# A fused layer kernel: the mixer stage's loads, stores and projection blocks in another order

## The chip, the cores and the metric

The kernel runs on one core of one Trainium2 chip. A core has five engines, each with an instruction queue of its own that is worked through in order: TensorE (PE, matrix products; the profile keeps its weight loads apart as PEld), VectorE (DVE), ScalarE (ACT), GpSimd (POOL) and SyncE (SP), which here issues every DMA. The metric is the device time of one execution in microseconds (us); of several executions the median is given.

## The reference

One layer of a diffusion backbone works on 128 context tokens and 2048 latent tokens, 1024 features each. After a modulated RMS norm, one projection feeds a short gated convolution (512 features) and a bidirectional mLSTM with four heads of 128; both meet in an output projection, and a gated feed-forward network (FFN) with a convolution follows. Cut to what the change touches:

```python
h = rmsnorm(x, norm1) * (1 + scale1) + shift1
sc_b, sc_c, sc_x, q, k, v, o, g = jnp.split(h @ w_in, idx, axis=-1)
u = (sc_c * sc_x).reshape(B, rows, row_len, D_CONV)
y_sc = sc_b * conv3(u, conv_sc_w, conv_sc_b, axis=2).reshape(B, T, D_CONV)
h_m, C, n, m = mlstm_bidir(heads(q), heads(k), heads(v), gates, C0, n0, m0)
h_m = h_m * lax.rsqrt(jnp.mean(h_m * h_m, axis=-1, keepdims=True) + EPS)
h_m = h_m * mh_norm.reshape(N_HEADS, HEAD_DIM).astype(jnp.float32)
h_m = h_m.reshape(B, T, D_MLSTM).astype(x.dtype) * jax.nn.sigmoid(o)
x = x + gate1 * (jnp.concatenate([y_sc, h_m], axis=-1) @ w_out)
h2 = rmsnorm(x, norm2) * (1 + scale2) + shift2
```

The mLSTM runs over 17 chunks of 128 tokens (chunk 0 is the context), forward and backward. Weights and activations are fp32; each product is made of three matmuls on high and low parts of its operands.

## The kernel before

Tokens stand in six blocks (0 to 5) of 384, the last of 256. A **block product** (`gemm`, lines 221 to 223) is one 128-row weight tile against one block: 8 slices times 3 matmuls, 24 in all, into one of two `acc` buffers. Its weight tile is loaded (line 119, two `wst` buffers), copied to its high part on ACT (line 127) and reduced to its low part on POOL in two halves (line 130).

The program's stages in order:

1. Start: modulation vectors, first norms, the v and gate projections of blocks 3 to 5 (`vg`), then block products of those three blocks for k, q, short convolution and o (`heads`, `shortconv`). Beside these, a generator `side` is advanced one step for each block product: `first_stats` sums the squares of blocks 0 to 2 on ACT and DVE (lines 177 to 181) and takes their inverse norms through PE, DVE and POOL (`inv_rms`, lines 144 to 148); then `mod_dve` makes 32 modulation vectors on DVE (two instructions of 1024 columns at line 661 and a small one at line 663 for each).
2. `vg` and the k heads of blocks 0 to 2 around the gate phase.
3. **Sums**: 34 units, one for each chunk and pair of heads, going backwards. A unit transposes k on PE (line 891), weighs v on DVE (895), multiplies on PE (902) and stores the state (918). Between units stand block products taken from a generator `fill`.
4. **Mix**: 34 units going forwards. `weave` writes one step for each unit; in it, stages of neighbouring units stand in a fixed order. For step i: `rows` (a 512 KB broadcast load of R, line 940) of unit i+2, `load` (k2, v2, q2, sb; lines 869, 874, 934) of unit i+1, the o gate load and the y store (869, 1031), the mask of unit i+1 on POOL (945), the products with R of unit i-1 on PE (976, 978), the scores of unit i (957), the transposes of unit i-3 (1021), and on DVE, ACT and POOL the denominators, head sums, norm and exponentials. After them `fill` gives block products.
5. The FFN: the out projection's last block products stand beside `sums`, which combines normalised rows for the FFN (spread at line 252, DVE at 272 to 284); then FFN up (1198 to 1200), then down (1352 to 1354).

`fill` in the kernel before is one chain: 12 block products for q, 12 for o, 36 for the short convolution of blocks 0 to 2 (12 weight tiles, three tiles at a time for three blocks each), and 32 of the 48 steps of `out_proj`. An `out_proj` step k loads the x row of step k+2 (line 553), multiplies (221 to 223), adds into the row on DVE (597), and at the beginning of step k+1 `close` stores that row (559), squares it on ACT (564) and adds the square on DVE (565). `next_y` brings in the y of the next blocks (504, 515, 516). `stats` (491 to 493) turns the summed squares of two blocks into inverse norms.

What sets the order: in Sums and before, a scheduler orders each engine's queue when the program is built. From the first Mix instruction to the end of `out_proj`, `in_order(first)` pins every engine to the order in which the code is written. `pa` gives two `acc` buffers; Mix has one PSUM bank for scores, two for y, and one (`st`) for transposes; k2 and q2 have three buffers, v2 and sb four, R four.

## Time and profile before

| | |
|---|---|
| Median of 3 runs | 2556.18 us (2555.6 to 2556.26) |
| The profiled execution | 2555.41 us, of which its span 2553.6 us |
| Mean granted TensorE clock | 0.987 of full speed |

Read the profile from PE: the page's first part gives each engine's busy share, its second part where in the span that share falls, and the fourth the chain that ended last. Of one execution, 1.8 us lie outside the span. Times in the span count from its first instruction.

### The profile page before, as it was taken

To read this page: it belongs to the slowest core of one execution; us is meant where nothing else is said; L and a number is where in the kernel's file an instruction comes from. 1 tells how busy PE (TensorE), PEld (TensorE's weight loads), DVE (VectorE), ACT (ScalarE), POOL (GpSimd) and SP (SyncE) were. 2 spreads that over 40 slices of the span, in tenths; PEclk is the share of its full clock that TensorE was granted. 3 is DMA by queue.
4 is the path that set the end of the run, shared out by engine and by line. 5 is a ranking of instruction groups with operands and counts; after the bars stand their busy time and mean duration, and the time that the engine had idled before them with its cause. 6 is when DMAs were issued, how large, how long until landed. Compare 5 with 4: busy or idle time off the path is not lost.

```text
span 2553.6 us, 42517 instructions
## 1 busy us (share of the span) xinstructions
PE 2469.7 (97%) x16127; PEld 2363.8 (93%) x16127; DVE 1664.1 (65%) x2738; ACT 1107.2 (43%) x2035; POOL 560.4 (22%) x467
## 2 busy tenths in 40 slices
PE   8999999999999889899999999899999999999998
PEld 8899999999999888899999999788888899999998
DVE  3992552322367666678678666877777786787586
ACT  4511143222255544455455444645555554443342
POOL 2531243111243333332112111121122100000000
PEclk9999999999999999999999999999999999999999
DMA  7772873255477776875225222522222277766674
GB/s 276 254 274 87 290 246 117 94 170 166 145 234 247 257 244 202 292 241 173 80 71 177 83 83 83 172 105 85 84 91 99 70 241 218 247 205 220 187 222 131
DMA packets 281423, 444.60 MB, mean 174 GB/s; under 512 B 23282, under 2 KB 206722, under 8 KB 279554
## 3 DMA queue, kind: packets, MB, share of 16 engines
q1 hardware_dynamic: 281218, 441.88, 53.0%
q8 instruction: 127, 2.08, 0.3%
q14 instruction: 78, 0.64, 0.1%
HBM read 335.31 MB, written 106.48 MB: 173 GB/s over the span
## 4 chain that ended last, share of the span: by engine, by line
PE 77%; DVE 9%; DMA 5%; issue 3%; ACT 3%; POOL 2%; SPq 1%; DVEq 0%; ACTq 0%; POOLq 0%
PE acc L221 7%; PE acc L223 7%; PE acc L222 7%; PE pa L1198 6%; PE pa L1200 6%; PE pa L1199 6%; PE d L1353 5%; PE d L1354 5%; PE d L1352 5%; PE pb L1198 3%; PE pb L1200 3%; PE pb L1199 3%; PE pc L1198 2%; PE pc L1199 2%; PE pc L1200 2%
## 5 line engine op out<-in xcount | busy, mean ns | idle before, releaser
L221 PE MATMUL acc<-hH,wh 128*128 128x384 f32 (+1 forms) x1536 | 515.6, 336 | 11.4 <-DVE row L597 11.1
L223 PE MATMUL acc<-hH,wl 128*128 128x384 f32 (+1 forms) x1536 | 507.5, 330 | 0.1
L222 PE MATMUL acc<-hL,wh 128*128 128x384 f32 (+1 forms) x1536 | 507.1, 330 | 0.0
L1352 PE MATMUL d<-bh,wh 128*128 128x272 f32 x1232 | 356.4, 290 | 0.7 <-ACT raw L1210 0.7
L1354 PE MATMUL d<-bh,wl 128*128 128x272 f32 x1232 | 356.8, 290 | 0.0
L1353 PE MATMUL d<-bl,wh 128*128 128x272 f32 x1232 | 356.2, 289 | 0.0
L1198 PE MATMUL pa<-tH,wh 128*128 128x288 f32 (+1 forms) x1056 | 347.8, 329 | 5.4 <-DVE raw L1212 2.9
L130 POOL TENSOR_TENSOR wl<-wst,wh 128x512 fp32r<-128x512 f32 (+1 forms) x160 | 236.6, 1500 | 518.8 <-ACT wh L127 497.3
L1200 PE MATMUL pa<-tH,wl 128*128 128x288 f32 (+1 forms) x1056 | 346.7, 328 | 1.0 <-DVE wl L331 1.0
L1199 PE MATMUL pa<-tL,wh 128*128 128x288 f32 (+1 forms) x1056 | 346.5, 328 | 0.0
L331 POOL TENSOR_TENSOR wl<-st,wh 128x512 fp32r<-128x512 f32 x132 | 185.7, 1408 | 695.5 <-ACT wh L330 655.2
L221 PEld LDWEIGHTS acc<-hH,wh 128*128 128x128 f32 x1536 | 293.3, 191 | 15.0 <-issue 10.5
L222 PEld LDWEIGHTS acc<-hL,wh 128*128 128x128 f32 x1536 | 292.8, 191 | 0.3 <-issue 0.2
L223 PEld LDWEIGHTS acc<-hH,wl 128*128 128x128 f32 x1536 | 292.2, 190 | 0.9 <-POOL wl L130 0.6
L1141 DVE SCALAR_TENSOR_TENSOR tt<-raw,fw,tt 128x127 f32<-128x127 f32 (+4 forms) x264 | 245.7, 952 | 3.7 <-ACT tt L1147 2.7
L1352 PEld LDWEIGHTS d<-bh,wh 128*128 128x128 f32 x1232 | 232.6, 189 | 1.3 <-ACT raw L1210 1.1
L1353 PEld LDWEIGHTS d<-bl,wh 128*128 128x128 f32 x1232 | 232.6, 189 | 0.2
L1354 PEld LDWEIGHTS d<-bh,wl 128*128 128x128 f32 x1232 | 232.5, 189 | 0.0
L1198 PEld LDWEIGHTS pa<-tH,wh 128*128 128x128 f32 x1056 | 198.4, 188 | 22.3 <-ACT c L1205 2.6
L1200 PEld LDWEIGHTS pa<-tH,wl 128*128 128x128 f32 x1056 | 199.0, 188 | 17.0 <-DVE wl L331 1.4
L1199 PEld LDWEIGHTS pa<-tL,wh 128*128 128x128 f32 x1056 | 198.6, 188 | 15.6
L330 ACT ACTIVATE wh<-s 128x512 fp32r<-128x512 f32 x176 | 110.8, 630 | 175.5 <-PE pc L1199 86.2
(243 smaller groups left out, 4834.0 us busy)
## 6 DMA issues: line engine op xcount, KB each, us to landing
st<-in_w_up SPq DMA_DIRECT2D x88, 512.0 KB, 3.8
us<-uD SPq DMA_DIRECT2D x48, 544.0 KB, 4.6
wst<-in_w_in SPq DMA_DIRECT2D x48, 512.0 KB, 3.7
uD<-tt SPq DMA_DIRECT2D x44, 544.0 KB, 2.7
R<-nD SPq DMA_DIRECT2D x34, 512.0 KB, 6.0
wm<-in_w_modr SPq DMA_DIRECT2D x32, 512.0 KB, 5.1
wst<-in_w_out SPq DMA_DIRECT2D x24, 512.0 KB, 5.6
st<-wsD SPq DMA_DIRECT2D x32, 384.0 KB, 3.3
```

Of the source, the lines that this page charges most:

```text
L130: G.tensor_sub(wl[:, a:a + n // 2], st[:, a:a + n // 2], wh[:, a:a + n // 2].bitcast(F32))
L221: PE.matmul(acc[:, :n], w_h, hH[:, k, :n], start=(k == 0), stop=False)
L222: PE.matmul(acc[:, :n], w_h, hL[:, k, :n], start=False, stop=False)
L223: PE.matmul(acc[:, :n], w_l, hH[:, k, :n], start=False, stop=(k == KT - 1))
L331: (G if on_pool else V).tensor_sub(wl, a, wh.bitcast(F32))
L1141: V.scalar_tensor_tensor(o, i, w, o, op0=ALU.mult, op1=ALU.add)
L1198: PE.matmul(acc, wh[:, w], rh, start=(kk == 0 and i in (0, 1, 5)), stop=False, skip_group_check=True)
L1199: PE.matmul(acc, wh[:, w], rl, start=False, stop=False, skip_group_check=True)
L1200: PE.matmul(acc, wl[:, w], rh, start=False, stop=(kk == 3), skip_group_check=True)
L1352: PE.matmul(acc, wh[:, c], uh, start=(kk == 0), stop=False)
L1353: PE.matmul(acc, wh[:, c], ul, start=False, stop=False)
L1354: PE.matmul(acc, wl[:, c], uh, start=False, stop=(kk == KH - 1))
```

## The change

Seven edits, most of them in Mix and around it.

- **o gate:** `head` multiplies the sigmoid by the head norm factor `mhn` on ACT (one more instruction for each of the 24 o block products); Mix then multiplies both heads in one DVE instruction (`third`) in place of two.
- **norm:** the mean's factor goes into the ACT square, and the addition of EPS moves from DVE to POOL.
- **Mix loads:** `load` stands two steps ahead, before `rows`.
- **Sums:** `load` two steps ahead, the second product two steps behind, three buffers for kT and vw.
- **Block products:** Sums gets the 24 of q and o, 0.65 for each step; Mix begins the short convolution and gets 1.6 for each step, where before Sums had one and Mix one with a second every third step from step 9 on. Sums goes from 38 to 24 block products and Mix from 48 to 60. Of `out_proj`, 26 steps stood in Mix and 22 behind it; now it is 24 and 24.
- **out_proj:** a row is stored and squared two steps after its product, and its square added a step later; `stats` five steps after a group's end rather than two.
- **first_stats:** three steps of `mod_dve` between the squares of a block and its inverse norm.

```diff
             S.activation(r[:, :n], acc[:, :n], func, scale=scale)
+            if func == AF.Sigmoid:
+                S.activation(r[:, :n], r[:, :n], AF.Copy, scale=mhn[:, h:h + 1])
             Q.dma_start(dst[h][:, t0:t0 + n], r[:, :n])
...
                 t0, n = BL[b]
-                ss = sss[b]
                 Q.dma_start(xD[m][:, t0:t0 + n], xr[:, :n])
                 if m == 0:
-                    S.activation(ss[:, :n], xr[:, :n], AF.Square)
+                    second = b in grps[1]
+                    sq = sss[b] = (rq if second else ssp).tile([P, 384], F32, name="cr" if second else "ss")
                 else:
                     sq = sqp.tile([P, 384], F32, name="sq")
-                    S.activation(sq[:, :n], xr[:, :n], AF.Square)
-                    V.tensor_add(ss[:, :n], ss[:, :n], sq[:, :n])
-
-            rows, got, behind, held, sss, past = [], [], [], [], {}, set()
+                S.activation(sq[:, :n], xr[:, :n], AF.Square)
+                return b, m, sq
+
+            def add(b, m, sq):
+                n = BL[b][1]
+                if m:
+                    V.tensor_add(sss[b][:, :n], sss[b][:, :n], sq[:, :n])
+
+            rows, got, behind, squared, held, sss, past = [], [], [], [], [], {}, set()
             for k in range(2):
...
                 grp, (t0, n) = grps[g], BL[b]
-                if k % 16 == 0:
-                    sss.update((b, ssp.tile([P, 384], F32, name="ss")) for b in grp)
-                    if g + 1 < len(grps):
-                        ny = next_y(grps[g + 1], (lambda: True, lambda b=grp[0]: (b, KT - 1) in past))
-                for x in behind:
-                    close(*x)
+                if k % 16 == 0 and g + 1 < len(grps):
+                    ny = next_y(grps[g + 1], (lambda: True, lambda b=grp[0]: (b, KT - 1) in past))
                 load_r(k + 2)
+                while squared:
+                    add(*squared.pop())
+                if len(behind) > 1:
+                    squared.append(close(*behind.pop(0)))
                 if k + 4 < len(steps):
...
                     del ws[:2]
-                if held and k == held[0] + 2:
-                    stats(*held[1:])
+                if held and k == held[0] + 5:
+                    stats(held[1], [sss[b] for b in held[1]])
                     held = []
...
                 past.add((b, m))
-                behind = [(b, m, xr)]
+                behind.append((b, m, xr))
                 if k % 16 == 15:
                     run(ny)
-                    if k == len(steps) - 1:
-                        close(*behind.pop())
-                        defer.append(lambda: stats(grp, [sss[b] for b in grp]))
-                    else:
-                        held = [k, grp, [sss[b] for b in grp]]
+                    held = [k, grp]
+                if k == len(steps) - 1:
+                    for x in squared + [close(*x) for x in behind]:
+                        add(*x)
+                    defer.append(lambda: stats(grp, [sss[b] for b in grp]))
                 yield
...
-            def first_stats():
+            def first_stats(mod):
+
                 for b in BA:
...
                     yield
+                    yield from islice(mod, 3)
                     inv_rms(ss, BL[b][1], rcol(b))
...
             late()
-            side = chain(first_stats(), mod_dve(), down_sums())
+            mod = mod_dve()
+            side = chain(first_stats(mod), mod, down_sums())
             run(vg((3,), hs, ws), prep(4))
...
                     PE.transpose(ps[:, h * P:(h + 1) * P], self.k2[:, h], ident)
-                self.kT = ms.tile([P, 256], F32, name="kT", bufs=2)
+                self.kT = ms.tile([P, 256], F32, name="kT", bufs=3)
                 S.activation(self.kT, ps[:, :256], AF.Copy)
-                self.vw = ms.tile([P, 2, 2, 129], F32, name="vw", bufs=2)
+                self.vw = ms.tile([P, 2, 2, 129], F32, name="vw", bufs=3)
                 V.tensor_tensor(self.vw, bc(self.v2[:, :, None, :], [P, 2, 2, 129]),
...
                 for h in range(2):
-                    S.activation(sj, hv[:, h], AF.Square, accum_out=ss[:, h:h + 1])
+                    S.activation(sj, hv[:, h], AF.Square, scale=QS, accum_out=ss[:, h:h + 1])
...
                 ss = self.ss
-                V.tensor_scalar(ss, ss, 1.0 / P, EPS, op0=ALU.mult, op1=ALU.add)
+                G.tensor_scalar(ss, ss, EPS, None, op0=ALU.add)
                 G.tensor_tensor(ss, ss, mhalf[:, :2], op=ALU.pow)
...
             def third(self):
-                hp, o2 = self.hp, self.o2
-                for h in range(2):
-                    V.scalar_tensor_tensor(o2[:, h], self.psT[:, h * P:(h + 1) * P], mhn[:, 2 * hp + h:2 * hp + h + 1], o2[:, h],
-                                           op0=ALU.mult, op1=ALU.mult)
+                o2 = self.o2
+                V.tensor_tensor(o2, self.psT[:, :256].rearrange("p (h t) -> p h t", h=2), o2, op=ALU.mult)
...
-        def weave(units, fill, extra, stages):
+        def weave(units, fill, rate, stages):
...
                 if -1 <= i < n + 3:
-                    next(fill, None)
-                    if extra and i >= 9 and i % extra == 0:
+                    for _ in range(int((i + 2) * rate) - int((i + 1) * rate)):
                         next(fill, None)
...
         outs = out_proj(((0, 1), (2, 3), (4, 5)), late, wo)
-        fill = chain(heads(BA, hs, 12, qD, AF.Copy, QS), heads(BA, hs, 20, oD, AF.Sigmoid, 1.0),
-                     shortconv(BA, hs, load_y, [I["w_out"][m] for m in range(2)], wo), islice(outs, 32))
+        fill = chain(heads(BA, hs, 12, qD, AF.Copy, QS), heads(BA, hs, 20, oD, AF.Sigmoid, 1.0))
         with tc.tile_pool(name="ms", bufs=1, side="right") as ms:
-            weave([Sums(c, hp) for c in range(NL - 1, -2, -1) for hp in range(2)], fill, 0,
-                  ((-1, "second"), (0, "first"), (1, "load")))
+            weave([Sums(c, hp) for c in range(NL - 1, -2, -1) for hp in range(2)], fill, 0.65,
+                  ((-2, "second"), (0, "first"), (2, "load")))
+        run(fill)
+        fill = chain(shortconv(BA, hs, load_y, [I["w_out"][m] for m in range(2)], wo), islice(outs, 37))
         mb = phr.enter_context(tc.tile_pool(name="mb", bufs=1, side="right"))
         first = len(nc.cur_bb.bb.instructions)
-        weave([Mix(c, hp) for c in range(-1, NL) for hp in range(2)], fill, 3,
-              ((2, "rows"), (1, "load"), (-2, "gate"), (-4, "last"), (1, "mask"),
+        weave([Mix(c, hp) for c in range(-1, NL) for hp in range(2)], fill, 1.6,
+              ((2, "load"), (2, "rows"), (-2, "gate"), (-4, "last"), (1, "mask"),
                (-1, "out"), (0, "scores"), (-3, "turn"), (0, "queries"), (-2, "norm"), (-1, "denom"), (0, "weigh"),
```

Three places where the order of the instructions changes:

**The inverse norms of blocks 0 to 2, on POOL, in the start stage.** `rc` is the inverse norm, `wl` a half of a weight's low part: two halves for each weight tile, a tile for three block products on PE. Before:

```order
L130 TENSOR_TENSOR wl<-wst,wh 128x512 x2
L148 TENSOR_TENSOR rc<-rc,mhalf 128x3
L130 TENSOR_TENSOR wl<-wst,wh 128x512 x2
L148 TENSOR_TENSOR rc<-rc,mhalf 128x3
L130 TENSOR_TENSOR wl<-wst,wh 128x512
L148 TENSOR_TENSOR rc<-rc,mhalf 128x3
```

After:

```order
L130 TENSOR_TENSOR wl<-wst,wh 128x512 x2
L148 TENSOR_TENSOR rc<-rc,mhalf 128x3
L130 TENSOR_TENSOR wl<-wst,wh 128x512 x4
L148 TENSOR_TENSOR rc<-rc,mhalf 128x3
L130 TENSOR_TENSOR wl<-wst,wh 128x512 x3
L148 TENSOR_TENSOR rc<-rc,mhalf 128x3
```

The three inverse norms stand further apart. On PE the three groups of sums of squares (line 144) stood after 2, 4 and 6 block products of the k heads, and now stand after 5, 10 and 15.

**The first weights of the short convolution of blocks 0 to 2, on SP, at the end of Sums.** `wst` is a weight tile, `row` a finished block product of o. Before, the third of these weights stands among the loads and stores of Sums, nine block products ahead of the convolution's first:

```order
L403 DMA oD_65<-row_5686 128x384
L918 DMA sD_67<-sb_5599 128x516
L874 DMA v2_5908<-vD_66 128x258
L119 DMA wst_6166<-in_w_in 128x1024
L403 DMA oD_65<-row_5740 128x384
```

After, all three stand behind the store of the last block product of Sums (row_6356, from acc_6331); the PE instruction behind acc_6331 is the first product with the weight wst_6385:

```order
L950 DMA R_6370<-nD_68 128x1024
L879 DMA k2_6372<-kD_63 128x2x128
L884 DMA v2_6374<-vD_66 128x258
L879 DMA q2_6376<-qD_64 128x2x128
L950 DMA R_6378<-nD_68 128x1024
L405 DMA oD_65<-row_6356 128x384
L119 DMA wst_6385<-in_w_in 128x1024
L119 DMA wst_6392<-in_w_in 128x1024
L119 DMA wst_6399<-in_w_in 128x1024
```

The weights moved from the middle of Sums to its end, behind a store.

**A step of Mix with an out projection block, on DVE.** `sq` is the squared row, `ss` their sum, `acc` the block product, `hL` the low part of the next y. Before:

```order
L966 TENSOR_TENSOR R_8669<-S_8913,R_8669 128x2x256
L1026 SCALAR_TENSOR_TENSOR o2_8770<-st_8916,mhn_133,o2_8770 128x128 x2
L1001 SCALAR_TENSOR_TENSOR hv_8931<-y_8904,den_8924,hv_8931 128x128 x2
L565 TENSOR_TENSOR ss_8510<-ss_8510,sq_8947 128x384
L516 TENSOR_TENSOR hL_8958<-xt_8859,hH_8957 128x384 x4
L597 SCALAR_TENSOR_TENSOR row_8820<-acc_8967,modT_85,row_8820 128x384
```

After:

```order
L976 TENSOR_TENSOR R_8943<-S_9188,R_8943 128x2x256
L1035 TENSOR_TENSOR o2_9035<-st_9191,o2_9035 128x256
L1011 SCALAR_TENSOR_TENSOR hv_9205<-y_9179,den_9199,hv_9205 128x128 x2
L572 TENSOR_TENSOR ss_8866<-ss_8866,sq_9122 128x384
L518 TENSOR_TENSOR hL_9130<-xt_9089,hH_9129 128x384 x4
L604 SCALAR_TENSOR_TENSOR row_9080<-acc_9239,modT_85,row_9080 128x384
```

The addition keeps its place ahead of the read of `acc`, but its square sq_9122 now belongs to an earlier step's ACT work (sq_8947 was made in the same step); and one instruction takes the place of two at the o gate.

## Prediction

> **What bounds the kernel now.** The page's first and fourth parts come first: busy time by engine, and the chain that ended last.
>
> ```profile
> span 2553.6 us, 42517 instructions
> ...
> PE 2469.7 (97%) x16127; PEld 2363.8 (93%) x16127; DVE 1664.1 (65%) x2738; ACT 1107.2 (43%) x2035; POOL 560.4 (22%) x467
> ...
> PE 77%; DVE 9%; DMA 5%; issue 3%; ACT 3%; POOL 2%; SPq 1%; DVEq 0%; ACTq 0%; POOLq 0%
> ```
>
> PE is busy for 2469.7 of 2553.6 us, so 84 us of idle time, and whatever PE loses at a lower clock, is all that this change can win; it takes no matmul away. Next comes busy time by stretch: the end of the start stage, Sums (two rows), Mix, the out projection behind it, and the FFN. The columns are the stretch, its length, busy time of PE, PEld, DVE, ACT, POOL, granted clock, DMA share and GB/s.
>
> ```profile
> 114.00:133.00 19.00, 13.56 (x75) 13.16 (x74) 18.86 (x34) 5.71 (x11) 8.04 (x5) 0.82 0.70 246
> 497.00:677.00 180.00, 180.00 (x1021) 174.62 (x1020) 47.59 (x107) 48.58 (x110) 32.84 (x22) 1.00 0.52 154
> 677.00:694.00 17.00, 17.00 (x98) 16.91 (x97) 4.16 (x9) 6.12 (x13) 2.58 (x2) 1.00 0.59 198
> 694.00:1005.00 311.00, 282.61 (x1825) 278.93 (x1823) 206.26 (x515) 154.87 (x489) 118.43 (x103) 0.97 0.75 238
> 1005.00:1121.00 116.00, 102.93 (x620) 99.09 (x620) 76.85 (x129) 49.91 (x95) 42.78 (x32) 0.94 0.80 270
> 1121.00:2553.00 1432.00, 1410.01 (x9358) 1322.25 (x9358) 1058.86 (x1468) 688.39 (x1027) 207.86 (x156) 0.99 0.44 144
> ```
>
> Sums has no idle PE time and can only lose. Mix has 28.4 us of it, the out projection 13.1, the start 5.4. The FFN's 22 us lie behind everything that changes; I leave them as they are. So the sum has four terms.
>
> **Term 1, the start: -8.1 us.** PE's groups, DVE's groups and PE's rows in the start stage, and the stretch in which the granted clock was 0.50:
>
> ```profile
> L144 PE MATMUL st<-ones,ss 128*128 128x1 f32 x18 | 3.0, 280 | 5.4 <-DVE modT L663 4.7 <-DVE rc L147 0.8
> ```
> ```profile
> L661 DVE SCALAR_TENSOR_TENSOR y<-wm,cB 128x1024 f32<-128x1024 f32 x25 | 34.4, 1375 | 0.3
> L181 DVE TENSOR_TENSOR ss<-ss,sq 128x384 f32<-128x384 f32 x15 | 11.8, 791 | 0.0
> ```
> ```profile
> 109.83 0.34 PE L221 MATMUL acc<-hH,wh 128*128 128x384 f32 x1
> ...
> 112.82 0.34 PE L223 MATMUL acc<-hH,wl 128*128 128x384 f32 x1
> ```
> ```profile
> 126.15:132.98 6.83, 5.31 (x19) 5.34 (x20) 6.73 (x12) 0.00 (x0) 0.96 (x1) 0.50 1.02 369
> ```
>
> PE waits 5.4 us for DVE at the sums of squares, and the 5.31 us of work behind it run at half the clock, which costs 2.7: together 8.1. Each sum now comes five block products after the one before, not two. The two PE rows stand 17 matmuls apart, 0.176 us each, so a block product of 24 takes 4.2 us, one of 256 tokens about two thirds of that (2.9), and five take 18.8 us on average. In that time DVE has, from an inverse norm to the last addition of the next block, seven additions (5.5 us) and six multiplications by the modulation weights (8.3): 13.8 us, a few small instructions beside. I take the whole 8.1. Bounds: -8.1, and -3 if DVE, which is full in this stretch, still comes 5 us late once.
>
> **Term 2, Mix: -31 us.** PE's groups between 694 and 1005 us with their idle time, and the half-clock stretches:
>
> ```profile
> L221 PE MATMUL acc<-hH,wh 128*128 128x384 f32 x361 | 126.5, 350 | 4.4 <-DVE row L597 4.4
> L978 PE MATMUL y<-v,R 128*128 128x129 f32 x272 | 52.9, 280 | 5.4 <-issue 2.6 <-DVE R L966 1.5 <-ACT hv L999 1.1
> ...
> L957 PE MATMUL S<-q,k 128*128 128x128 f32 x136 | 22.0, 287 | 15.3 <-DMA q<-qD 15.3
> ```
> ```profile
> 877.08:883.91 6.83, 4.17 (x15) 4.20 (x16) 6.76 (x15) 0.62 (x2) 3.21 (x3) 0.50 0.99 311
> 911.22:914.63 3.41, 3.41 (x14) 3.41 (x13) 3.41 (x4) 0.00 (x0) 3.41 (x4) 0.50 0.87 258
> 948.76:952.18 3.42, 3.42 (x18) 3.42 (x18) 0.73 (x3) 2.88 (x12) 0.00 (x0) 0.50 0.77 253
> 959.00:962.42 3.42, 3.17 (x10) 3.20 (x11) 3.34 (x13) 0.86 (x4) 0.74 (x1) 0.50 0.65 195
> 1006.79:1010.20 3.41, 3.41 (x13) 3.41 (x12) 2.96 (x3) 1.66 (x5) 2.84 (x2) 0.50 0.00 0
> ```
>
> The half-clock PE time is 17.6 us and costs 8.8; with 28.4 idle, Mix gives at most 37.2. More than half of the idle time is the scores' wait for q. The timeline shows one such wait:
>
> ```profile
> 870.41 0.75 SPq L869 DMA_DIRECT2D q<-qD  x1
> ...
> 879.74 0.55 PE L957 MATMUL S<-q,k 128*128 128x128 f32 x1 [6.74 <-DMA q<-qD]
> ```
>
> From issue to use it is 9.3 us, and one step of Mix is 311/34 = 9.1 us: a load one step ahead cannot make it when the DMA engines are full. SP also stands before it, for rows not yet written, and DVE for their squares:
>
> ```profile
> SPq L559 <- DVE row L597: 57.9, 11, 8.6
> ```
> ```profile
> L565 DVE TENSOR_TENSOR ss<-ss,sq 128x384 f32<-128x384 f32 x18 | 10.1, 558 | 44.0 <-ACT sq L564 44.0
> ```
>
> Waits of SP at the row stores: 57.9 us in 11, the longest 8.6. With loads two steps ahead (18 us) and a row stored two block products after it was made, both the 15.3 and SP's 57.9 should go. DVE's 44.0 us at the addition stand ahead of the next read of `acc`, and so of PE's 4.4; with the square a step old the addition finds it ready, and the 4.4 go. Behind these two waits come the clock stretches at 877, 911 and 959 (10.75 us, so 5.4). That is 25.1. Of the other 8.7 us (R, hv, issue) and the two remaining stretches (3.4) I let half go: 6. Bounds: everything (-37), and -19 (q's wait and half of what came with it).
>
> [...] The timeline before the stretch at 959:
>
> ```profile
> 959.25 0.66 PE L221 MATMUL acc<-hH,wh 128*128 128x384 f32 x1 [2.40 <-DVE row L597]
> ```
>
> [...]
>
> **Term 3, a new start-up wait between Sums and Mix: +10 us.** The first three short-convolution weights stand on SP behind the store of the last block product of Sums, and the next instruction of PE needs the first of them. The chain's links, from ACT's and POOL's groups in Sums, the page's DMA issues and SP's timeline:
>
> ```profile
> L402 ACT ACTIVATE row<-acc 128x384 f32<-128x384 f32 x21 | 10.2, 485 | 49.2 <-PE acc L223 49.2
> L127 ACT ACTIVATE wh<-wst 128x1024 fp32r<-128x1024 f32 x10 | 10.6, 1058 | 35.5 <-PE acc L222 32.2 <-issue 3.3
> L130 POOL TENSOR_TENSOR wl<-wst,wh 128x512 fp32r<-128x512 f32 x21 | 31.2, 1502 | 129.1 <-ACT wh L127 129.1
> ```
> ```profile
> wst<-in_w_in SPq DMA_DIRECT2D x48, 512.0 KB, 3.7
> ...
> wst<-in_w_out SPq DMA_DIRECT2D x24, 512.0 KB, 5.6
> ```
> ```profile
> 866.48 0.33 SPq L559 DMA_DIRECT2D xD<-row  x1
> ```
>
> From the end of that product: sigmoid 0.49, the new multiplication 0.49 (a Copy of the same size, priced as the sigmoid), two issues on SP 0.33 each: 1.6. Landing 3.7 (the first of the two rows, each with the KB of one transfer and the median us from issue to landing): 5.3. High part 1.06: 6.4. First half of the low part 1.50: 7.9 us until PE's third matmul of the next product. PE idles some 7.7 us, and the half-clock stretch behind it costs as the longest above did, 2.1. Since PE has no idle time at this place, nothing can be won here. Bounds: 0 if SP reaches the loads before the store, and +15.6 if landing takes q's 9.3.
>
> **Term 4, the out projection behind Mix: -4.5 us.** PE's groups between 1005 and 1121 us, and the half-clock stretch:
>
> ```profile
> L221 PE MATMUL acc<-hH,wh 128*128 128x384 f32 (+1 forms) x192 | 63.5, 331 | 7.0 <-DVE row L597 6.8
> L252 PE MATMUL st<-ident,rc 128*128 128x128 f32 (+3 forms) x24 | 5.2, 363 | 5.7 <-DVE rc L492 4.5 <-ACT rb L254 1.0 <-POOL rc L493 0.2
> ```
> ```profile
> 1057.99:1068.23 10.24, 6.17 (x25) 5.64 (x26) 3.62 (x8) 3.98 (x9) 3.01 (x3) 0.50 1.04 356
> ```
>
> `stats` three steps later leaves DVE and POOL time to finish, so of the 4.5 us of waiting at the spread I let 2.5 go, with half of the 3.1 of clock (1.5). Of 6.8 at `acc` 2 go. The last rows are stored and squared together at the very end, so that the FFN starts with less work left to cover its norms: +1.5. Bounds: -9 and +2.
>
> **What is hidden.** The new work on ACT (24 times 0.49, 12 us) lies in Sums, where ACT is busy 49 of 180 us. The norm's addition goes from DVE to POOL:
>
> ```profile
> L1008 DVE TENSOR_SCALAR hss<-hss 128x2 f32<-128x2 f32 x34 | 14.2, 418 | 0.4
> L1009 POOL TENSOR_TENSOR hss<-hss,mhalf 128x2 f32<-128x2 f32 x34 | 24.9, 732 | 77.2 <-DVE hss L1008 74.6 <-DMA yD<-o 2.5
> ```
>
> DVE loses 14.2 us; POOL gains at most 34 times 0.73, 25 us, and at least DVE's 14, beside 118 of 311 busy. It stands between two units' stages a step apart, so I cost it at nothing; uncovered, it would be as much as 25. The o gate's single instruction saves DVE a little more. The block products only change place: the 14 taken from Sums cost PE the same in Mix.
>
> **Sum.** -8.1 - 31 + 10 - 4.5 = -33.6 on the profiled execution's 2555.4: 2521.8. The median of the runs is 0.8 above that execution, so I forecast **2522**.
>
> **Rivals.** *No start-up wait* (SP's queue reaches the weights in time): 10 less, 2512. Against it stands the order on SP. *The loads stay late*: DMA shares of 0.99, 0.87 and 0.77 stand beside the first three half-clock stretches of Mix, and 12 more block products in Mix bring more weights. If the transfers' rate is what binds, loads issued earlier only queue longer; term 2 shrinks to about -12, giving 2541; against it, the share over all of Mix is 0.75. *DVE still comes late at `acc`*: the waits for `row` in terms 2 and 4 stay (4.4, their 1.6 of clock, 2): 2530. *Slower*: SP is one queue, and two steps ahead the loads wait at the head of each step until unit i-1's k2 and q2 buffers (three of each) are free; the weights queue behind. SP's longest stand in Mix now:
>
> ```profile
> SPq L429 <- DVE yr L474: 26.2, 8, 8.8
> ```
>
> A weight has a quad of blocks (two steps and a half, 23 us) from its issue, less landing 5.6 (the out projection's row above), two high parts (2.1) and four halves of low parts (6.0): 9 us of slack. SP would have to stand longer than its 8.8 by some 4 us at each; then ten weight pairs late by 5 us with their half clock make +50, 2570. Against it, the 57.9 us at row stores go.
>
> **How the numbers follow.** Forecast 0.62; no start-up wait 0.13; loads late 0.10; DVE late 0.10; slower 0.05. The terms' bounds put the forecast's own range at 2508 to 2536; with the late loads it reaches 2544. About 0.2%, 5 us, is what a measurement of this kernel can tell from no change. Faster by more than that: 0.91 (all cases but the last, less 0.04 of the late loads with an unlucky third term); within: 0.04; slower: 0.05.
>
> **What would show it.** Term 1: no idle time at L144 and no half clock near 126. Term 2: no wait of the scores for q, of PE for `row`, or of SP at row stores. Term 3: one gap of 7 to 8 us on PE where Sums ends, released by POOL or ACT at the weight; a gap over 14 us would make the loads' landing the cause. Term 4: the spread's wait near 2 us. Wrong altogether if PE's waits in Mix turn to weights.

## The result and the profile after

| | median us | executions | ratio to the kernel before |
|---|---|---|---|
| before | 2556.22 | 2555.6 to 2559.78 (4) | |
| after | 2542.04 | 2538.4 to 2547.02 (4) | 0.9943 [0.9924, 0.9962] |

The change gains 14.2 us where 34 were forecast. The time lies outside the forecast's own range of 2508 to 2536 us; it is inside only the 2544 that the rival with late loads was given. The profiled execution of the changed kernel took 2547.02 us (span 2545.2), the longest of its four, so its trace accounts for 8.4 of the 14.2 us. The trace says where PE loses time here, and the runs say what each part is worth.

First the busy time by stretch of the changed kernel, with the columns of the prediction's table: the end of the start stage, the end of Sums, Mix, and the out projection up to the FFN's first product.

```profile
114.00:133.00 19.00, 19.00 (x129) 19.00 (x128) 18.72 (x31) 3.73 (x7) 6.27 (x4) 1.00 0.72 269
...
618.00:637.50 19.50, 10.87 (x45) 10.04 (x44) 0.00 (x0) 6.94 (x11) 6.85 (x6) 0.74 0.65 221
637.50:983.00 345.50, 332.55 (x2139) 330.93 (x2138) 208.83 (x467) 167.90 (x511) 144.02 (x149) 0.99 0.71 227
983.00:1106.40 123.40, 105.42 (x638) 103.09 (x637) 84.08 (x129) 47.33 (x90) 42.52 (x32) 0.95 0.71 241
```

The start has no PE idle time any more. Sums, which had none, loses 8.6 us at its end. Mix idles for 12.9 us where it had 28.4, and the out projection for 18.0 where it had 13.1. The half-clock stretches between 618 us and the start of the FFN:

```profile
626.21:636.46 10.25, 6.31 (x19) 5.80 (x20) 0.00 (x0) 3.79 (x7) 4.99 (x4) 0.50 0.42 150
841.25:844.67 3.42, 3.09 (x14) 3.09 (x15) 1.59 (x5) 2.90 (x13) 0.94 (x2) 0.50 1.02 309
899.28:902.70 3.42, 3.42 (x13) 3.42 (x12) 3.35 (x11) 1.38 (x7) 0.52 (x1) 0.50 0.96 328
950.48:953.90 3.42, 3.42 (x12) 3.42 (x11) 2.84 (x9) 2.33 (x10) 0.73 (x2) 0.50 0.85 260
1028.98:1032.40 3.42, 3.42 (x13) 3.42 (x12) 2.81 (x7) 1.84 (x4) 0.00 (x0) 0.50 0.55 178
1052.87:1056.29 3.42, 3.42 (x13) 3.42 (x12) 0.00 (x0) 0.62 (x2) 0.00 (x0) 0.50 0.97 321
1066.53:1069.94 3.41, 3.41 (x12) 3.41 (x11) 3.41 (x4) 1.29 (x2) 2.97 (x3) 0.50 1.05 390
1104.08:1110.91 6.83, 4.50 (x19) 4.53 (x20) 6.16 (x10) 4.81 (x8) 0.00 (x0) 0.50 0.80 288
```

At the granted clock of 0.50, half of PE's busy time in a stretch is put down as what it cost, an estimate that comes out a little high (in the stretch at 1028.98 us the matmuls of 384 columns start 0.32 us apart, just behind it 0.17): 3.2 us at the end of Sums, 5.0 in Mix (three stretches), 5.1 in the out projection (three), 2.3 at the start of the FFN. PE's groups in Mix:

```profile
L221 PE MATMUL acc<-hH,wh 128*128 128x384 f32 x466 | 161.4, 346 | 6.3 <-DVE row L604 6.3
...
L988 PE MATMUL y<-v,R 128*128 128x129 f32 x272 | 52.9, 280 | 3.5 <-DVE R L976 3.5
...
L986 PE MATMUL y<-sf,R 128*128 128x129 f32 x128 | 25.0, 277 | 2.8 <-DVE R L972 2.8
L967 PE MATMUL S<-q,k 128*128 128x128 f32 x136 | 20.7, 275 | 0.0
```

The scores (L967) no longer wait for q, but the products wait for the row on DVE longer than before: 6.3 us, where it was 4.4. Between Mix and the FFN:

```profile
L221 PE MATMUL acc<-hH,wh 128*128 128x384 f32 (+1 forms) x200 | 66.6, 333 | 8.8 <-DVE row L604 8.2 <-ACT sq L566 0.4
...
L252 PE MATMUL st<-ident,rc 128*128 128x128 f32 (+3 forms) x24 | 3.7, 285 | 1.9 <-ACT rb L254 1.0 <-POOL rc L495 0.7 <-DVE rc L494 0.3
L1206 PE MATMUL pa<-tH,wh 128*128 128x288 f32 x5 | 2.3, 470 | 7.3 <-issue 7.3
```

The spread (L252) waits 1.9 us instead of 5.7. The FFN's first product (L1206) now starts after 7.3 us of idle time that was not there before; "issue" means that the profile names no releaser. Last, two groups of DVE in Mix and a wait of SP's queue in Mix (us in total, times, longest):

```profile
L518 DVE TENSOR_TENSOR hL<-xt,hH 128x384 fp32r<-128x384 f32 x35 | 33.7, 1021 | 14.7 <-ACT hH L517 14.7
...
L572 DVE TENSOR_TENSOR ss<-ss,sq 128x384 f32<-128x384 f32 x14 | 8.2, 585 | 4.4 <-ACT sq L566 4.4
```
```profile
SPq L560 <- DVE row L604: 12.8, 6, 6.4
```

DVE's wait for squares fell from 44.0 to 4.4 us, SP's at the row stores from 57.9 to 12.8. SP did not become free by it: in Mix it now stands 51 us ahead of k and q loads (line 879) and 54 us ahead of the short convolution's stores (line 431). That is the stand which the slower rival spoke of, but no PE wait in Mix names a weight.

### The profile page after: what moved, and what is told of

Read it like the earlier page. It is cut to its first block, busy times and chain, and to the rows that moved or that the text cites. A ratio compares the mean times of both kernels' runs of the same rounds, so it can differ in the third digit from the quotient of the medians.

```text
span 2545.2 us, 42525 instructions
## 1 busy us (share of the span) xinstructions
PE 2464.8 (97%) x16127; PEld 2360.4 (93%) x16127; DVE 1664.6 (65%) x2670; ACT 1122.8 (44%) x2059; POOL 573.7 (23%) x501
## 4 chain that ended last, share of the span: by engine, by line
PE 68%; DVE 5%; DMA 4%; issue 2%; ACT 1%; POOL 0%; SPq 0%; DVEq 0%; ACTq 0%; POOLq 0%
PE pa L1206 7%; PE pa L1208 6%; PE pa L1207 6%; PE d L1361 5%; PE d L1362 5%; PE d L1360 5%; PE acc L221 4%; PE acc L223 4%; PE acc L222 4%; PE pb L1206 3%; PE pb L1207 3%; PE pb L1208 3%; PE pc L1206 2%; PE pc L1207 2%; PE pc L1208 2%
## 5 line engine op out<-in xcount | busy, mean ns | idle before, releaser
L1206 PE MATMUL pa<-tH,wh 128*128 128x288 f32 (+1 forms) x1056 | 348.7, 330 | 12.1 <-issue 7.3
L130 POOL TENSOR_TENSOR wl<-wst,wh 128x512 fp32r<-128x512 f32 (+1 forms) x160 | 236.5, 1501 | 419.2 <-ACT wh L127 373.1
L1206 PEld LDWEIGHTS pa<-tH,wh 128*128 128x128 f32 x1056 | 199.3, 189 | 28.8 <-issue 8.3
```

The costliest lines, as they stand in the source:

```text
L130: G.tensor_sub(wl[:, a:a + n // 2], st[:, a:a + n // 2], wh[:, a:a + n // 2].bitcast(F32))
L1206: PE.matmul(acc, wh[:, w], rh, start=(kk == 0 and i in (0, 1, 5)), stop=False, skip_group_check=True)
```

## The experiments

Each kernel was run beside the kernel before on the same chip, but not all on one chip. Medians of before differ by up to 3.4 us between the groups of runs, so the ratios are what is compared; where medians are given, they can be off by as much.

| kernel | median us | ratio to before, 95% interval |
|---|---|---|
| after: first weights earlier | 2528.07 | 0.9885 [0.9868, 0.9901] |
| after: next y behind the row | 2532.26 | 0.9900 [0.9885, 0.9915] |
| after: more cover for the FFN | 2534.23 | 0.9909 [0.9895, 0.9924] |
| after: these three | 2512.74 | 0.9824 [0.9810, 0.9839] |
| before: first_stats alone | 2547.16 | 0.9972 [0.9960, 0.9983] |
| before: Mix loads alone | 2556.45 | 1.0001 [0.9992, 1.0009] |
| after: Mix loads as before | 2541.92 | 0.9941 [0.9927, 0.9954] |
| after: rows closed as before | 2550.87 | 0.9982 [0.9973, 0.9991] |
| before: rows closed later alone | 2543.41 | 0.9958 [0.9944, 0.9972] |
| the three edits, blocks dealt as before | 2526.82 | 0.9904 [0.9889, 0.9919] |
| after: norm and o gate as before | 2541.45 | 0.9953 [0.9940, 0.9966] |
| the three edits, 1.75 blocks a step | 2519.97 | 0.9855 [0.9835, 0.9874] |

### The wait at the end of Sums

The timeline of the changed kernel there, from ACT, SP and PE:

```profile
621.56 0.49 ACT L402 ACTIVATE row<-acc 128x384 f32<-128x384 f32 x1 [3.46 <-PE acc L223]
622.08 0.61 ACT L404 ACTIVATE row<-row,mhn 128x384 f32<-128x384 f32 x1
...
628.64 1.06 ACT L127 ACTIVATE wh<-wst 128x1024 fp32r<-128x1024 f32 x1 [1.51 <-DMA wst<-in_w_in]
```
```profile
622.72 0.32 SPq L405 DMA_DIRECT2D oD<-row  x1
623.14 0.95 SPq L119 DMA_DIRECT2D wst<-in_w_in  x2
```
```profile
629.75 0.69 PE L221 MATMUL acc<-hH,wh 128*128 128x384 f32 x1 [8.23 <-ACT wh L127]
...
631.16 0.69 PE L223 MATMUL acc<-hH,wl 128*128 128x384 f32 x1 [0.40 <-POOL wl L130]
```

These are the links of the prediction one by one: sigmoid, multiplication, store, load, high part, PE. The load is issued at 623.14, its high part starts at 628.64. The experiment takes these loads earlier:

```diff
+        sc = shortconv(BA, hs, load_y, [I["w_out"][m] for m in range(2)], wo)
+        def first_w():
+            next(sc)
+            return
+            yield
+        ho = heads(BA, hs, 20, oD, AF.Sigmoid, 1.0)
-        fill = chain(heads(BA, hs, 12, qD, AF.Copy, QS), heads(BA, hs, 20, oD, AF.Sigmoid, 1.0))
+        fill = chain(heads(BA, hs, 12, qD, AF.Copy, QS), islice(ho, 10), first_w(), ho)
...
             ws += [load_w(next(todo)) for _ in range(3)]
+            if then:
+                yield
```

> The changed kernel with the first three short-convolution weights taken while the last o blocks still run, ahead of the pinned order. Theory (start-up wait: the loads stand behind the last store on SP): the gap of 8.6 us on PE where Sums ends and the half clock behind it, 3.2 us, both go, so about 12 us less than the changed kernel's 2542: 2530. Rival (PE waits there for something other than the order on SP): the gap stays at 7 us or more, the time within 3 us of 2542.

The time is 2528.07, a ratio of 0.9885, 14 us below the changed kernel. PE has no idle time from 612 to 628 us (16.00 of 16.00 us busy), and Mix keeps its 6.5 us at the row. So the wait came from the place of the loads on SP, and cost 12 us by the trace and 14 by the medians.

### What holds DVE at the row

In Mix of the changed kernel DVE works on the next y ahead of the row, while POOL makes a weight's low part. DVE's and POOL's rows:

```profile
892.60 4.92 DVE L518 TENSOR_TENSOR hL<-xt,hH 128x384 fp32r<-128x384 f32 x4 [3.71 <-ACT hH L517]
897.45 0.60 DVE L604 SCALAR_TENSOR_TENSOR row<-acc,modT,row 128x384 f32<-128x384 f32 x1
```
```profile
892.23 2.87 POOL L130 TENSOR_TENSOR wl<-wst,wh 128x512 fp32r<-128x512 f32 x2 [6.81 <-ACT wh L127]
895.07 1.57 POOL L955 TENSOR_TENSOR R<-R,maskN 128x512 f32<-128x512 f32 x1
```

The read of `acc` (L604) stands behind four low parts, and these first wait 3.71 us for ACT. The experiment moves them behind it:

```diff
-                if k % 16 >= 5:
-                    next(ny, None)
                 acc = gemm(w, early[b], n)
...
                 behind.append((b, m, xr))
+                if k % 16 >= 5:
+                    next(ny, None)
```

> The changed kernel with the work on the next y (high part on ACT, low part on DVE) placed behind the addition of the row in its step instead of ahead of it. Theory (DVE reads the accumulator late because four low parts of the next y, 1.2 us each, stand ahead of the read and wait for ACT): PE's waits for row in Mix (2.7 and 3.7 us) and the one of 3.9 us at 1024 us go, with half-clock time of some 4 us: 10 to 14 us less, about 2530. Rival (DVE is simply full there, so the wait moves to R or to the scores): PE's idle time in Mix stays at 11 us or more and the time within 4 us of 2542.

The time is 2532.26 (0.9900), 10 us less. PE's groups in Mix of this kernel:

```profile
L221 PE MATMUL acc<-hH,wh 128*128 128x384 f32 x465 | 159.7, 343 | 0.0
...
L988 PE MATMUL y<-v,R 128*128 128x129 f32 x272 | 53.2, 281 | 4.8 <-DVE R L976 3.8 <-issue 1.0
```

The wait at the row in Mix is gone, and R's grew by 1.3 us only. Behind Mix PE still waits 6.8 us for rows, where it was 8.2, though no longer 3.9 us at once: the longest wait is 1.9.

### The gap ahead of the FFN

Two numbers change in the changed kernel:

```diff
-                if held and k == held[0] + 5:
+                if held and k == held[0] + 3:
...
-islice(outs, 37)
+islice(outs, 35)
```

The late inverse norms force five more of the out projection's steps ahead of the FFN's second group of sums (37 in the slice, where 32 stood), so that one block product instead of four was left to cover their end. Here three are left.

> The changed kernel with the inverse norms three steps after a group's end instead of five, and two out projection steps fewer ahead of the sums for the FFN, so that three instead of one block product stands behind them. Theory (the gap of 7.3 us ahead of the FFN is a lack of cover): the gap falls to 0 or 1 us and the half clock behind it (2.3 us) goes: 8 to 9.5 us less, some 2 us given back at the spread: about 2535. Rival (the gap is a chain of transfers that starts later with the last rows): the gap stays above 5 us, 2542.

The time is 2534.23 (0.9909), 8 us less. The row of the FFN's first product in the stretch from 984 to 1110 us:

```profile
L1206 PE MATMUL pa<-tH,wh 128*128 128x288 f32 x16 | 4.8, 300 | 0.6 <-issue 0.6
```

The gap fell from 7.3 to 0.6 us without a loss at the spread, which waits 1.9 us as in the changed kernel. What was late is the chain of the FFN's sums, and DVE's rows in the changed kernel show how it reached PE:

```profile
1100.30 1.36 DVE L313 TENSOR_TENSOR tL<-F,tH 128x1152 fp32r<-128x1152 f32 x1 [6.36 <-ACT tH L312]
...
1105.83 0.48 DVE L604 SCALAR_TENSOR_TENSOR row<-acc,modT,row 128x256 f32<-128x256 f32 x1
```

DVE stood 6.4 us for the FFN's first operand (L313), with the reads of the last block products queued behind it. The last of these reads ends at 1106.31 us, and PE starts at 1106.41; in the kernel before (1121.18 and 1121.28) and in this one the FFN's first product also starts 0.1 us after the last read. By this timing PE's "issue" was a wait for DVE, and what covers it is the number of block products behind the sums. The edit changes the norms' place too, and the two were not tried apart.

### The three together

> The three edits together. If the three waits are separate, the gains add up: 2542 - 12 - 11 - 7 = 2512. If they share a cause (transfers or DVE being full), the sum comes out at half of it or less: 2527 or more.

The time is 2512.74 (0.9824 [0.9810, 0.9839]), 29 us below the changed kernel, where the three gains of 14, 10 and 8 add up to 32. So the three waits are separate but for some 3 us. This version is 43 to 45 us below the kernel before.

### The first term alone

One line goes into the kernel before:

```diff
                     ss = squares(b, load_x(b, I["x"], xp, "xt", 2))
                     yield
+                    yield from islice(mod, 3)
                     inv_rms(ss, BL[b][1], rcol(b))
```

> The kernel before with the three steps between squares and inverse norms alone. Theory (the first term of the prediction): the waits at the sums of squares, 5.4 us, and the half clock at 126 us, 2.7, go: 8 less than 2556.2, so 2548. Rival (DVE is full there and comes late at the next place): 0 to 3 less, 2553 or more, with new PE idle time before 390 us.

The time is 2547.16, by its ratio 7 us less [4, 10]. PE's row at the sums of squares, between 90 and 140 us:

```profile
L144 PE MATMUL st<-ones,ss 128*128 128x1 f32 x12 | 1.4, 236 | 0.0
```

Of the rival's new idle time little came: between 140 and 390 us PE idles for 1.6 us, where it idled for none.

### The loads of Mix

One kernel takes the new order of the loads alone into the kernel before, another takes it back in the changed kernel:

```diff
-              ((2, "rows"), (1, "load"), (-2, "gate"), (-4, "last"), (1, "mask"),
+              ((2, "load"), (2, "rows"), (-2, "gate"), (-4, "last"), (1, "mask"),
```

> The kernel before with the Mix loads two steps ahead, ahead of the R rows, alone. Theory (one step is too short a lead for q): the scores' wait of 15.3 us goes and with it the half clock at 877 and 911 us, 3.8: 19 less, 2537. Rival (the DMA engines are full, so the wait moves to R, the weights or a later q): 6 less at most, 2550 or more.

> The changed kernel with the Mix loads one step ahead again, behind the R rows. Theory (the lead is what q needs): the scores wait for q again, 10 to 15 us with half clock behind, 2555 to 2561. Rival (storing a row two blocks later already freed SP's queue, so that one step would have done): q's wait stays below 3 us, 2540 to 2546.

Both rivals' times: 2556.45 (1.0001) with the longer lead in the kernel before, 2541.92 (0.9941) without it in the changed one. The lead is worth nothing measurable in either, as both rivals said. Mix of the kernel before with the longer lead, PE's groups and DVE's squares:

```profile
L978 PE MATMUL y<-v,R 128*128 128x129 f32 x272 | 55.4, 291 | 11.0 <-issue 9.3 <-DVE R L966 1.5
...
L976 PE MATMUL y<-sf,R 128*128 128x129 f32 x128 | 26.1, 287 | 7.5 <-DVE R L962 4.7 <-DMA v<-vD 2.9
L957 PE MATMUL S<-q,k 128*128 128x128 f32 x136 | 21.4, 281 | 0.0
```
```profile
L565 DVE TENSOR_TENSOR ss<-ss,sq 128x384 f32<-128x384 f32 x18 | 10.1, 559 | 44.0 <-ACT sq L564 44.0
```

The scores' 15.3 us are gone, and the next products wait that much longer, at R (5.4 to 11.0 and 1.3 to 7.5 us) and at the row (4.4 to 7.0). Mix idles for 29.1 us, where it was 28.4. Half of the wait at R has no releaser by name ("issue"), but PE goes on as DVE finishes R:

```profile
921.96 0.68 DVE L966 TENSOR_TENSOR R<-S,R 128x512 f32<-128x512 f32 x1
```
```profile
922.74 0.46 PE L978 MATMUL y<-v,R 128*128 128x129 f32 x2 [2.45 <-issue]
```

The other gaps of over 1 us at line 978 also end 0.1 us after DVE's R. DVE still stands 44.0 us for squares. So PE met DVE's delay one instruction later, and not the full DMA engines of the first rival: by the profile 2.9 us of these waits are for a transfer (v), and the DMA share over this Mix was 0.73. In the changed kernel with the load one step ahead, q is not waited for either:

```profile
L967 PE MATMUL S<-q,k 128*128 128x128 f32 x136 | 21.2, 279 | 0.0
```

### The closing of rows

This edit closes the rows of the changed kernel as before:

```diff
-                while squared:
-                    add(*squared.pop())
-                if len(behind) > 1:
-                    squared.append(close(*behind.pop(0)))
+                if behind:
+                    add(*close(*behind.pop(0)))
```

> The changed kernel with each row stored, squared and added at the beginning of the next out projection step, as before; norms still five steps behind. Theory (waiting for the square held DVE, and SP at the store): PE's waits for row in Mix and behind it grow by 2 to 6 us with their half clock, 2546 to 2552, and SP stands at the row stores some 50 us again. Rival (the low parts of the next y hold DVE at the same place anyway): within 3 us of 2542.

The time is 2550.87 (0.9982), 9 to 10 us more than the changed kernel. DVE's group and SP's wait in its Mix:

```profile
L572 DVE TENSOR_TENSOR ss<-ss,sq 128x384 f32<-128x384 f32 x14 | 8.3, 591 | 30.5 <-ACT sq L566 30.5
```
```profile
SPq L560 <- DVE row L602: 71.1, 17, 9.2
```

Both stands come back. The waits did not come where I expected them: at the row 4.5 us instead of 6.3, at R 11.8 instead of 6.3. The same edit put into the kernel before, with the inverse norms three steps behind and 35 in the slice:

> The kernel before with rows stored and squared two steps after their product and the square added a step later (inverse norms three steps after a group, three more out projection steps ahead of the FFN's sums); loads still one step ahead. New theory (DVE standing for a square of the same step, 45 us in Mix, is the root; SP's stand at the row store and q's late arrival follow from it): the wait for q goes with it, Mix loses 12 to 16 us less, the wait at the spread gets shorter too: 2535 to 2541. Rival (q also needs the longer lead): q's wait stays at 6 us or more, 2546 or more.

The time is 2543.41 (0.9958), 10.7 us less by the ratio: a smaller gain than the new theory gave, a larger one than the rival's. Its Mix, from PE, DVE and SP:

```profile
L962 PE MATMUL S<-q,k 128*128 128x128 f32 x136 | 21.2, 280 | 3.1 <-DMA q<-qD 3.1
```
```profile
L570 DVE TENSOR_TENSOR ss<-ss,sq 128x384 f32<-128x384 f32 x14 | 9.0, 644 | 6.4 <-ACT sq L564 6.4
```
```profile
SPq L558 <- DVE row L602: 12.8, 2, 6.4
```

With q loaded one step ahead as before, its wait falls from 15.3 to 3.1 us, with DVE's wait for squares and SP's stand. The late q followed from these; which of the two stands it was, DVE's or SP's, was not tried apart. The kernel before shows the two in a row ahead of the load that it issued at 870.41 us:

```profile
865.24 0.56 DVE L565 TENSOR_TENSOR ss<-ss,sq 128x384 f32<-128x384 f32 x1 [5.73 <-ACT sq L564]
```

DVE finishes its row behind this addition at 866.44, and SP's store of it (line 559) goes out at 866.48, ahead of R, k, v and q. What is left of PE's waits in Mix stands at R (7.6 us) and at the row (6.4). In the changed kernel the low parts were what held the row; here that was not tried.

### The dealing of the block products

```diff
-        fill = chain(heads(BA, hs, 12, qD, AF.Copy, QS), islice(ho, 10), first_w(), ho)
+        fill = chain(heads(BA, hs, 12, qD, AF.Copy, QS), islice(ho, 10), first_w(), ho, sc, islice(outs, 35))
...
-            weave([Sums(c, hp) for c in range(NL - 1, -2, -1) for hp in range(2)], fill, 0.65,
+            weave([Sums(c, hp) for c in range(NL - 1, -2, -1) for hp in range(2)], fill, 1.0,
...
-        weave([Mix(c, hp) for c in range(-1, NL) for hp in range(2)], fill, 1.6,
+        weave([Mix(c, hp) for c in range(-1, NL) for hp in range(2)], fill, 1.0,
...
+                    if extra and i >= 9 and i % extra == 0:
+                        next(fill, None)
```

> The faster version with all three edits (2512.7), but the block products dealt out as before: the short convolution begins in Sums, one block product a step there, in Mix one a step and a second every third step from the tenth. Theory (a Mix step with 1.6 block products covers DVE's work better than one with 1.3): PE's idle time in Mix rises from 8.6 to 15 us or more, 2519 to 2526. Rival (the dealing as such changes nothing, PE's work only stands elsewhere): within 3 us of 2512.7.

The time is 2526.82 (0.9904): more than with the new dealing by 14 us if the medians are compared, by 20 if the ratios are. By the traces, with idle time and half clock added, Mix loses 21.3 us instead of 11.1, and the out projection behind it 3.6 more. Mix with the old dealing:

```profile
685.60:982.70 297.10, 281.84 (x1826) 278.25 (x1826) 188.68 (x449) 154.78 (x491) 129.69 (x137) 0.98 0.78 248
```

And with the new one:

```profile
626.00:966.00 340.00, 331.45 (x2141) 329.42 (x2140) 201.11 (x465) 168.34 (x514) 140.24 (x147) 0.99 0.72 232
```

With 12 block products more, Mix idles for 8.6 us instead of 15.3: PE waits less for R (7.6 us, where it is 12.1) and at the transposes (0.9, where it is 3.2), while PE's idle time from 400 us to the start of Mix, with fewer block products there, is 1.0 us instead of 0.8. More is not better still. At 1.75 instead of 1.6 for each step:

```diff
-        weave([Mix(c, hp) for c in range(-1, NL) for hp in range(2)], fill, 1.6,
+        weave([Mix(c, hp) for c in range(-1, NL) for hp in range(2)], fill, 1.75,
```

> The faster version with all three edits (2512.7), with 1.75 instead of 1.6 block products for each Mix step, so that six more of the out projection's stand in Mix and six fewer behind it. Theory (each block product more in a Mix step covers DVE and what hangs on it): Mix loses 8 us or less where it lost 11, and behind it PE has less to cover the FFN's sums with: 2507 to 2513. Rival (the cover is enough at 1.6, and the six are missed behind Mix): the loss behind Mix grows by 5 us or more, 2516 to 2524.

The time is 2519.97 (0.9855), 7 us more. Mix and what lies behind it, and PE's longest wait behind it:

```profile
630.60:988.50 357.90, 352.52 (x2258) 350.49 (x2257) 220.39 (x483) 173.21 (x524) 147.15 (x150) 0.99 0.71 229
988.50:1086.80 98.30, 83.99 (x527) 82.37 (x526) 64.13 (x114) 43.03 (x82) 36.58 (x28) 0.94 0.81 277
```
```profile
PE st L495 <- DVE ss L574: 5.2, 1, 5.2
```

Mix idles 5.4 us, 3.2 less; with the half clock it loses 8.8 where it lost 11.1, a little short of the theory. The part behind it idles 14.3 instead of 9.1, as the rival said: PE now comes to the last sums of squares before DVE.

### Norm and o gate

The edit takes back the factor at the o gate, the square's scale and the addition on POOL.

```diff
-                S.activation(r[:, :n], r[:, :n], AF.Copy, scale=mhn[:, h:h + 1])
...
-                G.tensor_scalar(ss, ss, EPS, None, op0=ALU.add)
+                V.tensor_scalar(ss, ss, 1.0 / P, EPS, op0=ALU.mult, op1=ALU.add)
...
-                V.tensor_tensor(o2, self.psT[:, :256].rearrange("p (h t) -> p h t", h=2), o2, op=ALU.mult)
+                    V.scalar_tensor_tensor(o2[:, h], self.psT[:, h * P:(h + 1) * P], mhn[:, 2 * hp + h:2 * hp + h + 1], o2[:, h],
+                                           op0=ALU.mult, op1=ALU.mult)
```

> The changed kernel with the norm's addition back on DVE and the head norm factor back in two DVE instructions at the o gate. Prediction (these edits are hidden): within 3 us of 2542, with DVE in Mix busy some 20 us more. Rival (DVE's queue is what PE waits for at the rows, so some of those 20 us reach PE): 2546 or more.

The time is 2541.45 (0.9953, against 0.9943): no difference that shows. Its Mix:

```profile
640.00:985.00 345.00, 332.72 (x2139) 330.99 (x2139) 212.67 (x534) 168.50 (x514) 133.19 (x115) 0.99 0.71 228
```

DVE is busy 212.7 us, only 3.8 more than in the changed kernel, not 20; POOL is busy 10.8 less. DVE's groups show where the rest went. The o gate and the norm do bring 18 us (19.8 instead of 13.7, and 12.1), but with POOL less busy two other groups take 11 us less: the states (line 995 of the changed kernel) take 24.8 us instead of 32.7, and the low parts 30.6 instead of 33.7.

## Why the prediction was wrong

The direction was right, the size was not. By the trace the four terms miss by 27 us in all: 14 in term 4, 12 in term 2 and 2 in term 3.

*Term 1, the start: right.* Forecast -8.1; the trace shows all of it gone, and the run of this edit alone gained 7 [4, 10].

*Term 2, Mix: forecast -31, by the trace -19.* Before, 28.4 us of idle time and 8.8 of clock; after, 12.9 and 5.0. (The 8.8 hold the stretch at 1006.79 us, 1.7, which the prediction counted in Mix though it lies behind its end.) The step that failed is the sentence that credits the loads: "a load one step ahead cannot make it when the DMA engines are full". q's 15.3 us were the largest term of the sum, and moving the loads alone gained nothing, in either kernel. q came late because its load stood on SP behind a row store, which waited for DVE, which waited for ACT's square (5.73 us ahead of the load issued at 870.41; with the rows closed later alone q's 15.3 us fell to 3.1); and where q came in time PE waited for R instead (11.0 and 7.5 us at its products, where it was 5.4 and 1.3), since DVE was late all the same (44.0 us for squares in both). What paid was the later closing of rows, 10 us (0.9982 against 0.9943 when it is undone; 0.9958 alone, of which the traces put 9 us in Mix).

A second step of this term failed: "with the square a step old the addition finds it ready, and the 4.4 go". The first half held (44.0 to 4.4 us), the second did not, since the low parts of the next y stand on DVE between the addition and the read, and wait for ACT as well (3.71 us in the row at 892.60). The rows of the order showed them there (`hL`, four of them, ahead of the row). The mechanism of the rival with DVE late at `acc` came true in Mix, though not its time, 2530. The rival with late loads gave 2541, which is nearly what was measured, but by luck: q is not waited for.

*The dealing: forecast nothing, worth 14 us or more* in the version where it was tried. "The block products only change place" counted PE's work and left out what that work covers. By the trace this is 10 of Mix's 19 us, if it is worth the same in the changed kernel as in the version of the experiment. Undoing the closing of rows put 7 us back into Mix (24.9 us of idle time and clock, where it was 17.9).

*Term 3, the wait at the end of Sums: right in its mechanism and nearly in its size.* Forecast +10; measured 8.6 idle and 3.2 of clock, 11.8. The high part started 5.5 us after the load's issue, where the sum had 3.7 for the landing.

*Term 4, the out projection: forecast -4.5, by the trace +9.2.* Before, 13.1 us of idle time and 3.1 of clock; after, 18.0 and 7.4. The term mis-sized is the start of the FFN: "less work left to cover its norms: +1.5" cost 7.3 of idle time and 2.3 of clock, 9.6. The 1.5 was worked out from no row. The change leaves one block product behind the sums where four stood, and these could have been priced, at 4.2 us each or 2.9 for the block of 256 tokens. The sentence also looked to the closing of the last rows, where the runs show the sums' chain on DVE. The spread did as forecast (5.7 to 1.9 us, -3.8). The wait at the row rose from 6.8 to 8.2 us instead of falling by 2, and the cost of half clock ahead of the FFN rose from 3.1 to 5.1.

*Hidden work: right in the time, not in the account.* Norm and o gate show no difference, but they free 3.8 us of DVE in Mix, not the 14.2 and more that were counted, since other groups of DVE took longer while POOL had more work (the states 32.7 us where they take 24.8 with POOL busy 10.8 less, the low parts 33.7 where they take 30.6).

*The sum.* 2521.8 and 0.8 make 2522.6, where 2522 was put down. The terms' bounds, added up with the same 0.8, give 2502 to 2552; the narrower range of 2508 to 2536 was not worked out from them, and the measured time lies between the two upper ends.

Of the four terms the measured sum is -8 - 19 + 12 + 9 = -6 us on the trace of the longest execution, which itself is 8 below the one before. The medians differ by 14. The difference between 8 and 14 lies in the spread of the changed kernel's executions, 2538 to 2547. In this trace the FFN, which the change leaves alone, loses some 5 us more than before (24 of idle time and 8 of clock, where it was 23 and 5); why is open.

## What to carry to other kernels

When the longest wait on the bounding engine names a transfer, follow that transfer's queue back to what it stood behind before giving it more lead: here the wait for q was DVE's delay by way of SP, and removing it alone only moved the wait (29.1 us of idle time in Mix, where it was 28.4). Price cover in both directions: an edit that spaces out dependent steps also moves where the next stage may begin, and block products that "only move" bring cover to one stage and take it from another (the new dealing won at least 14 us at 1.6 a step and lost 7 of them at 1.75). Where code is pinned from some instruction on, load what its first instruction needs before the pin (14 us here).

## What the runs showed of the hardware

Four of DVE's low parts took 4.92 us beside POOL's work and 1.97 without it, 2.5 times as long. A row of DVE in the changed kernel's Mix while POOL was idle, to be laid beside the row at 892.60 us above, the same four instructions beside POOL's L130 and L955:

```profile
823.23 1.97 DVE L518 TENSOR_TENSOR hL<-xt,hH 128x384 fp32r<-128x384 f32 x4 [2.36 <-ACT hH L517]
```

That is 0.49 against 1.23 us for one, 2.95 us more for the four, and they stand on DVE ahead of the row that PE waits for until 898.20 us (2.66 us of idle time), though POOL is named by no wait there. Single instructions show how. Between the start of Mix and the FFN DVE makes 40 low parts of 384 columns: 23 took 0.54 to 0.56 us, 17 took 1.34 to 1.65. Each of the 17 began while POOL ran an instruction of 512 columns (L130 or L955), and ended 0.41 or 0.42 us after that one ended; beside POOL's instructions of two columns none was slow. So by these rows a low part waits for the end of the POOL instruction and does not merely run at a lower rate. DVE's read of `acc` from PSUM (L604, 384 columns) took 0.60 to 0.62 us with POOL busy or idle. What ties the low parts to POOL is not shown, and no run moved POOL's work away, so what it costs in time is not shown either.

In the same trace idle times of PE of under 3 us stood ahead of stretches of some 3.4 us with a granted clock of 0.50: 2.80 us for R, and 1.11 more, at the one from 841.25 us, 2.66 us at the row ahead of the one from 899.28, and 1.86 us at the row ahead of the one from 1066.53. An idle time of 1.87 us that ended at 1083.85 was followed by none: from there to 1095 us the granted clock was 1.00. So here the length of an idle time alone did not decide.
